# Narrow and wide matmuls of a seven-product up-projection, paired by channel tile

## The chip, the core and the metric

One core of a Trainium2 chip runs the whole block as one program. TensorE (PE in the profile) multiplies; its weight loads have a row of their own (PEld). VectorE (DVE), ScalarE (ACT) and GpSimd (POOL) work on the elements, SyncE (SP) issues most transfers. The metric is the device time of one execution in microseconds, as the median of three runs.

## The reference

A diffusion block on 512 latent tokens of width 2048: a mixer of two recurrent head groups, then a SwiGLU MLP with a 3x3 depthwise convolution on the gate branch, and a final norm. The change touches the MLP's up-projection only:

```python
def conv_ffn(h, rows, cols, w_up, conv_w, conv_b, w_down):
    b, t, _ = h.shape
    u = jnp.einsum('btd,df->btf', h, w_up)
    u_gate, u_val = jnp.split(u, 2, axis=-1)
    g = lax.conv_general_dilated(u_gate.reshape(b, rows, cols, D_FF), conv_w[:, :, None, :], ...)
    g = g.reshape(b, t, D_FF) + conv_b
    return jnp.einsum('btf,fd->btd', jax.nn.silu(g) * u_val, w_down)
```

Here t is 512, d is 2048 and f is 5504, which is 43 channel tiles of 128.

## The kernel before

**Two-part numbers.** To get float32 results from single-pass matmuls, each operand is split into a high part (a copy on ScalarE, line 90, that rounds) and a low part (the rest, a subtraction on VectorE, line 91). A product is then the sum of three: high x high, high x low and low x high.

**Seven products.** `up_seven(f)` makes the gate and the value of channel tile f, for f from 4 to 42. It halves the 16 tiles of 128 input channels (KH = 8 in a half), the 512 tokens (TH = 256 in a half) and the outputs (gate and value), and multiplies the resulting 2x2 blocks with seven products in place of eight, in Winograd's form: sums of token blocks are made once for the whole stage (`token_sums`), sums of weight blocks for every tile, by accumulating transfers and by two additions on VectorE. A product n takes a weight block of 8 pieces of 128x128, split into `wh` and `wl`, as the stationary operand, and as the moving one `operands[n](k)`, which holds the high part of 256 tokens in its first half and the low part in its second. So there are two kinds of matmul: a **narrow** one, `wl` against the high part (256 columns into the first half of the result), and a **wide** one, `wh` against both parts (512 columns into both halves). The halves are added later, with the combination of the products. In the profile the narrow ones read `lo_q` and the wide ones `hi_q`. The program issues all eight narrow ones, then all eight wide ones, into the same bank of PSUM (`x`, `w` or `v`).

**Order around it.** Tiles 4 to 38 and 40, 36 in all, also run a down block (`dn`, 48 matmuls of 512 columns) between their sixth and seventh product; 39, 41 and 42 don't. The product order is 0, 1, 3, 2, 5, 4, down block, 6 in the first kind and 0 to 6 in the second. Each engine takes its instructions in program order, which a scheduler sets from the program's text, its dependences and its priorities; splits and evacuations have high priority.

**Buffers.** The high parts rotate through three buffers in this stage (`hi_tile`), the low parts through two (`wlo`, tag `lo`), and the down block's weights use the same ones. A buffer is free when the last matmul that reads it is done.

The convolution (`conv`) is nine taps per tile, the first on ScalarE, eight on VectorE (line 1207). All matmuls of this stage show line 98, that of a helper.

Of the kernel before, what the change touches and what calls it, by code (L numbers as in the profile page):

```python
# [70 lines left out]
def block_kernel(ctx: ExitStack, tc: tile.TileContext, a: dict, out: bass.AP):  # L71
# [8 lines left out]
    def sub(o, x, y):  # L80
        V.tensor_tensor(out=o, in0=x, in1=y, op=ALU.subtract)
# [4 lines left out]
    def add(o, x, y):  # L86
        V.tensor_tensor(out=o, in0=x, in1=y, op=ALU.add)

    def split(hi, lo, x):
        split_ins[0] = S.copy(hi, x).ins  # L90
        return V.tensor_tensor(out=lo, in0=x, in1=hi.bitcast(F32), op=ALU.subtract).ins  # L91
# [5 lines left out]
    def mm(*args, **kw):  # L97
        ins = PE.matmul(*args, **kw)  # L98
        if pinned[0]:
            tc.keep_in_program_order(ins)  # L100
# [37 lines left out]
    def acc(name, shape=(P, T)):  # L138
        return psA.tile(list(shape), F32, name=name, tag="acc")

    def psb(name, shape=(P, T)):
        return psB.tile(list(shape), F32, name=name, tag="psb")
# [52 lines left out]
    def hi_tile(name, n):  # L195

        turn[0] += 1
        if third[0] and turn[0] % 3 == 0:
            return third[0].tile([P, 2 * T], F32R, name=name, tag="hi3")[:, 0:n]
        return whi.tile([P, n], F32R, name=name, tag="hi")  # L200
# [852 lines left out]
    for g in range(4):  # L1053
        if g:
            accs = unit(a["w_gates"][g], f"ga{g}", *hx)
        for i in range(4):
            k = 4 * g + i
# [53 lines left out]
    for n in range(4):  # L1111
        accs = unit(a["w_out"][n], f"wo{n}", yh, yl)
        with tc.high_priority():
            for i in range(4):
                k = 4 * n + i
# [12 lines left out]
    KH, TH = KT // 2, T // 2  # L1128
# [39 lines left out]
    def neg_add(o, x, y):  # L1168
        V.scalar_tensor_tensor(out=o, in0=x, scalar=-1.0, in1=y, op0=ALU.mult, op1=ALU.subtract)
# [27 lines left out]
    def conv(f, pad, val):  # L1197

        t = stage[1] if f < FIRST and f % 2 else tp.tile([P, T], F32, name=f"cv{f}", tag="cv")
        t3 = t.rearrange("p (r c) -> p r c", c=GW)  # L1200
        for tap in range(9):
            src = pad[:, tap // 3 : tap // 3 + ROWS, tap % 3 : tap % 3 + GW]
            w = cwt[:, f, tap : tap + 1]
            if tap == 0:
                S.activation(t3, src, AF.Identity, scale=w, bias=cbt[:, f : f + 1])  # L1205
            else:
                V.scalar_tensor_tensor(out=t3, in0=src, scalar=w, in1=t3, op0=ALU.mult, op1=ALU.add)  # L1207
        S.activation(t, t, AF.Silu)
        mul(t, t, val)
        gs[f] = [ytile(2 * (f % 8) + i, f"g{'hl'[i]}{f}", dtype=F32R) for i in range(2)]  # L1210
        split(*gs[f], t)

    def vtile(f):
        return stage[0] if f < FIRST and f % 2 else tp.tile([P, T], F32, name=f"val{f}", tag="val")
# [29 lines left out]
    def up_seven(f):  # L1244

        def load(q, i, j, **kw):
            eng = G if kw else nc.sync
            eng.dma_start(q, a["w_up"][f - FIRST, i, j].rearrange("p k c -> p (k c)"), **kw)  # L1248

        def block(n):  # L1250
            return wraw.tile([P, KH * P], F32, name=f"q{f}_{n}", tag="raw")

        s1, s3 = spare[0][:, f % 2, :], spare[1][:, 0, :]
        load(s1, 1, 0)
        a11 = block(0)
        load(a11, 0, 0)
        load(s1, 1, 1, accum_op=ALU.add)
        load(s3, 1, 0)
        a12 = block(1)
        load(a12, 0, 1)  # L1260
        load(s3, 0, 0, accum_op=ALU.add)

        def product(n, src, o, first):
            wh = hi_tile(f"hi_q{f}_{n}", KH * P)
            wl = wlo.tile([P, KH * P], F32R, name=f"lo_q{f}_{n}", tag="lo")
            with tc.high_priority():
                split(wh, wl, src)
            cs = [slice(P * k, P * k + P) for k in range(KH)]
            for k in range(KH):
                mm(o[:, 0, :], wl[:, cs[k]], operands[n](k)[:, 0], start=first and k == 0, stop=False,  # L1270
                   skip_group_check=True)
            for k in range(KH):
                mm(o, wh[:, cs[k]], operands[n](k), start=False, stop=k == KH - 1, skip_group_check=True)

        def rows(x):
            return x.rearrange("p (r c) -> p r c", c=GW)

        x = psb(f"x{f}", (P, 2, TH))
        w, v = (acc(f"{n}{f}", (P, 2, TH)) for n in "wv")
        pad, val = pads[f % 2], vtile(f)  # L1280

        def part(name, tag):
            return fp.tile([P, 2, TH], F32, name=f"{name}{f}", tag=tag)

        p1 = part("p1", "pa")

        def c11():
            add(p1, w, p1)
            add(pad[:, 1 : ROWS // 2 + 1, 1 : GW + 1], rows(p1[:, 0]), rows(p1[:, 1]))

        def c12():
            add(u2, v, u2)
            add(pad[:, ROWS // 2 + 1 : ROWS + 1, 1 : GW + 1], rows(u2[:, 0]), rows(u2[:, 1]))

        def c22():
            neg_add(p5, x, p5)
            add(val[:, hi], p5[:, 0], p5[:, 1])

        def c21():
            S.activation(val[:, lo], x[:, 0], AF.Copy, scale=-1.0)  # L1300
            sub(val[:, lo], val[:, lo], x[:, 1])

        def step(n, src, o, after):
            product(n, src, o, n in (0, 1, 3))
            with tc.high_priority():
                after()

        step(0, a11, x, lambda: S.copy(p1, x))
        step(1, a12, w, c11)
        with tc.high_priority():  # L1310
            add(a11, s1, a11)
            add(a12, a12, a11)
        p5, u2 = part("p5", "pa"), part("u2", "u2")
        steps = [(2, a11, x, lambda: S.copy(u2, x)), (3, s1, v, lambda: S.copy(p5, v)), (4, s3, x, c22), (5, a12, v, c12)]  # L1314
        for n in (1, 0, 3, 2) if f in DOWN else range(4):
            step(*steps[n])
        if f in DOWN:
            down_block(GROUPS[min(f // 4, 9) - 1], DOWN[f])
        a22 = block(2)
        load(a22, 1, 1)  # L1320
        step(6, a22, x, c21)
        conv(f, pad, val)
# [12 lines left out]
    def down_block(fs, blk):  # L1335
        accs = down_products(fs, blk)
        with tc.high_priority():
            for i in range(4):
                k = 4 * blk + i
                S.activation(stage[i], accs[i], AF.Copy, scale=modc[5][:, k : k + 1])  # L1340
                G.dma_start(x2d[k], stage[i], accum_op=ALU.add)
# [147 lines left out]
```

## Time and profile before

| what | us |
|---|---|
| median of 3 runs (lowest, highest) | 2479.32 (2476.03, 2481.27) |
| the profiled execution | 2478.88 |
| its span, first to last instruction | 2476.8 |
| VectorE's low splits of `q` buffers in the stage from 1240 to 2380, 191 of them | 230.6 busy |
| VectorE's eight taps of a tile in the same stretch, 306 of them | 229.2 busy |
| TensorE's idle time in the same stretch | 0.7 |

The stage with seven products a tile fills the stretch from about 1228 to 2380 us of the span. In the profile, a row of the time line gives the start, the time it lasts, the engine, the line, the operation and the tiles it writes and reads, and a count where equal rows are merged. A matmul's time there includes the fill and drain that the next one overlaps, so the distance of two starts, and not the duration, says what it costs.

### The profile page before, as it was taken

To read this page: it belongs to the slowest core of one execution; us is meant where nothing else is said; L and a number is where in the kernel's file an instruction comes from. 1 tells how busy PE (TensorE), PEld (TensorE's weight loads), DVE (VectorE), ACT (ScalarE), POOL (GpSimd) and SP (SyncE) were. 2 spreads that over 40 slices of the span, in tenths; PEclk is the share of its full clock that TensorE was granted. 3 is DMA by queue.
4 is the path that set the end of the run, shared out by engine and by line. 5 is a ranking of instruction groups with operands and counts; after the bars stand their busy time and mean duration, and the time that the engine had idled before them with its cause. 6 is when DMAs were issued, how large, how long until landed. Compare 5 with 4: busy or idle time off the path is not lost.

```text
span 2476.8 us, 35238 instructions
## 1 busy us (share of the span) xinstructions
PE 2439.1 (98%) x13610; PEld 2110.3 (85%) x13610; DVE 1752.0 (71%) x2472; ACT 1120.1 (45%) x1664; POOL 370.3 (15%) x362
## 2 busy tenths in 40 slices
PE   7999999999999999999999999999999999999998
PEld 4888899989998888888888888888888888888887
DVE  5566766555555688867887777777777777777884
ACT  4224544322323444435455555555555555555553
POOL 0000000000000344540011111111111111111101
PEclk9999999999999999999999999999999999999999
DMA  9751112124343878862588888888888888888762
GB/s 371 279 189 52 35 43 77 60 86 136 128 137 102 265 267 291 281 204 90 145 186 190 192 190 194 194 195 190 194 190 192 187 189 190 193 190 191 181 205 69
DMA packets 137913, 429.68 MB, mean 173 GB/s; under 512 B 15505, under 2 KB 19985, under 8 KB 137745
## 3 DMA queue, kind: packets, MB, share of 16 engines
q1 hardware_dynamic: 104688, 348.24, 42.8%
q0 software_dynamic: 31968, 78.66, 20.1%
q8 instruction: 107, 1.75, 0.3%
q10 hardware_dynamic: 1088, 0.52, 0.1%
q14 instruction: 62, 0.50, 0.1%
HBM read 381.22 MB, written 46.14 MB: 173 GB/s over the span
## 4 chain that ended last, share of the span: by engine, by line
PE 91%; issue 3%; DVE 3%; DMA 1%; ACT 0%; POOL 0%; SPq 0%; POOLq 0%; DVEq 0%; ACTq 0%
PE a L98 18%; PE x L98 17%; PE dn L98 16%; PE v L98 9%; PE wo L98 7%; PE ga L98 7%; PE w L98 4%; PE po L98 4%; PE u L98 4%; PE ps_m L98 1%; PE sl L98 1%; PE cst L98 1%; PE mc L325 1%; DMA xl<-in_xT 0%; PE s L98 0%
## 5 line engine op out<-in xcount | busy, mean ns | idle before, releaser
L91 DVE TENSOR_TENSOR lo_q<-q,hi_q 128x1024 fp32r<-128x1024 f32 x195 | 235.4, 1223 | 143.1 <-ACT spare L1340 117.6
L90 ACT CAST hi_q<-q 128x1024 fp32r<-128x1024 f32 x195 | 205.2, 1053 | 230.4 <-PE dn L98 162.0
L98 PE MATMUL dn<-gh,lo_d 128*128 128x512 f32 x660 | 257.6, 390 | 0.0
L98 PE MATMUL dn<-gl,hi_d 128*128 128x512 f32 x660 | 257.5, 390 | 0.0
L98 PE MATMUL dn<-gh,hi_d 128*128 128x512 f32 x660 | 257.5, 390 | 0.0
L1207 DVE SCALAR_TENSOR_TENSOR cv<-pad,cwt,cv 128x512 f32<-128x512 f32 x328 | 246.6, 752 | 6.3 <-ACT cv L1205 0.5
L98 PE MATMUL x<-bt,hi_q 128*128 128x512 f32 x936 | 235.4, 394 | 0.0
L98 PEld LDWEIGHTS x<-bt,hi_q 128*128 128x128 f32 x936 | 167.7, 188 | 30.7
L1248 POOL DMA_DIRECT2D spare<-in_w_up x78 | 68.7, 883 | 728.6 <-DMA spare<-in_w_up 647.4
L314 POOL TENSOR_TENSOR sumg_m<-sumg_m,raw_m 128x512 f32<-128x512 f32 x74 | 124.1, 1677 | 198.7 <-ACT raw_m L313 172.3
L98 PE MATMUL a<-hi_h,hTh 128*128 128x256 f32 x512 | 149.1, 291 | 0.0
L91 DVE TENSOR_TENSOR lo_d<-raw_d,hi_d 128x1024 fp32r<-128x1024 f32 x84 | 101.3, 1206 | 66.4 <-ACT hi_d L90 52.0
L306 DVE SCALAR_TENSOR_TENSOR sum_m<-raw_m,csil,sum_m 128x512 f32<-128x512 f32 x112 | 145.5, 1299 | 1.3
L98 PEld LDWEIGHTS dn<-gl,hi_d 128*128 128x128 f32 x660 | 124.0, 188 | 26.2 <-DVE gl L91 0.2
L98 PEld LDWEIGHTS dn<-gh,hi_d 128*128 128x128 f32 x660 | 123.9, 188 | 26.3 <-ACT gh L90 0.4
L98 PEld LDWEIGHTS dn<-gh,lo_d 128*128 128x128 f32 x660 | 124.0, 188 | 26.1
L98 PE MATMUL a<-lo_h,hTh 128*128 128x256 f32 x512 | 145.0, 283 | 0.0
L98 PE MATMUL a<-hi_h,hTl 128*128 128x256 f32 x512 | 145.0, 283 | 0.0
L91 DVE TENSOR_TENSOR lo_q<-spare,hi_q 128x1024 fp32r<-128x1024 f32 x78 | 95.3, 1222 | 56.3 <-ACT hi_q L90 56.3
L98 PEld LDWEIGHTS x<-bt,lo_q 128*128 128x128 f32 x936 | 125.7, 188 | 10.3 <-ACT u L1314 1.1
L90 ACT CAST hi_h<-raw_h 128x1024 fp32r<-128x1024 f32 x64 | 67.0, 1047 | 137.9 <-PE a L98 129.7
L98 PE MATMUL x<-bt,lo_q 128*128 128x256 f32 x936 | 128.2, 279 | 0.7 <-ACT u L1314 0.7
(371 smaller groups left out, 5872.3 us busy)
## 6 DMA issues: line engine op xcount, KB each, us to landing
raw_m<-in_w_mod SPq DMA_DIRECT2D x192, 512.0 KB, 4.9
q<-in_w_up SPq DMA_DIRECT2D x117, 512.0 KB, 4.7
raw_d<-in_w_down SPq DMA_DIRECT2D x81, 512.0 KB, 4.1
spare<-in_w_up SPq DMA_DIRECT2D x78, 512.0 KB, 4.5
spare<-in_w_up POOLq DMA_DIRECT2D x78, 512.0 KB, 7.3
raw_h<-in_w_heads SPq DMA_DIRECT2D x64, 512.0 KB, 3.5
x2d<-stage POOLq DMA_DIRECT2D x72, 256.0 KB, 5.1
x2d<-spare POOLq DMA_DIRECT2D x72, 256.0 KB, 5.1
```

The costliest lines, as they stand in the source:

```text
L90: split_ins[0] = S.copy(hi, x).ins
L91: return V.tensor_tensor(out=lo, in0=x, in1=hi.bitcast(F32), op=ALU.subtract).ins
L98: ins = PE.matmul(*args, **kw)
L306: V.scalar_tensor_tensor(out=parts["v"], in0=raw[:, 0, :], scalar=ce, in1=parts["v"], op0=ALU.mult, op1=ALU.add)
L314: G.tensor_tensor(out=parts["g"], in0=parts["g"], in1=raw[:, 1, :], op=ALU.add)
L325: tc.keep_in_program_order(PE.matmul(ps[:, i : i + 1], po[:, P * i : P * i + P], cst[:, C_ONE : C_ONE + 1], start=True, stop=True))
L1207: V.scalar_tensor_tensor(out=t3, in0=src, scalar=w, in1=t3, op0=ALU.mult, op1=ALU.add)
L1248: eng.dma_start(q, a["w_up"][f - FIRST, i, j].rearrange("p k c -> p (k c)"), **kw)
```

## The change

The second `for k` line goes away, so that the loop body issues the narrow matmul of piece k and then the wide one of the same piece:

```diff
             for k in range(KH):
                 mm(o[:, 0, :], wl[:, cs[k]], operands[n](k)[:, 0], start=first and k == 0, stop=False,
                    skip_group_check=True)
-            for k in range(KH):
                 mm(o, wh[:, cs[k]], operands[n](k), start=False, stop=k == KH - 1, skip_group_check=True)
```

The number of instructions of each kind is the same. What moves is their order. On TensorE, at the start of tile 13 (the stage's tenth), there stands before, with `b00` and `b1` as token operands and the number behind `q` as the tile and the product:

```order
L98 MATMUL x13_12847<-b00_9578,lo_q13_0_12853 128x256 x8
L98 MATMUL x13_12847<-b00_9578,hi_q13_0_12852 128x512 x8
L98 MATMUL w13_12848<-b1_9580,lo_q13_1_12874 128x256 x8
L98 MATMUL w13_12848<-b1_9580,hi_q13_1_12873 128x512 x8
L98 MATMUL v13_12849<-bt0_9581,lo_q13_3_12900 128x256 x8
```

On TensorE at the same place there now stands, for the first half of product 0:

```order
L98 MATMUL x13_12847<-b00_9578,lo_q13_0_12853 128x256
L98 MATMUL x13_12847<-b00_9578,hi_q13_0_12852 128x512
L98 MATMUL x13_12847<-b00_9578,lo_q13_0_12853 128x256
L98 MATMUL x13_12847<-b00_9578,hi_q13_0_12852 128x512
L98 MATMUL x13_12847<-b00_9578,lo_q13_0_12853 128x256
L98 MATMUL x13_12847<-b00_9578,hi_q13_0_12852 128x512
```

The runs of eight have become single rows that alternate; the order of the products is the same as before in every tile but tile 4, where product 5 now stands ahead of product 4's last pair.

VectorE's order moves too, since the scheduler sees the low buffer in use for longer. From the start of tile 13, before (`q13_0` and `q13_1` are the raw weight blocks, `spare` a sum of two, `val12` and `cv12` the value and the convolution of the tile ahead):

```order
L91 TENSOR_TENSOR lo_q13_0_12853<-q13_0_12840,hi_q13_0_12852 128x1024
L91 TENSOR_TENSOR lo_q13_1_12874<-q13_1_12844,hi_q13_1_12873 128x1024
L87 TENSOR_TENSOR q13_0_12840<-spare_10516,q13_0_12840 128x1024
L81 TENSOR_TENSOR val12_12592<-val12_12592,x12_12589 128x256
L87 TENSOR_TENSOR q13_1_12844<-q13_1_12844,q13_0_12840 128x1024
L91 TENSOR_TENSOR lo_q13_3_12900<-spare_10516,hi_q13_3_12899 128x1024
L84 TENSOR_TENSOR cv12_12823<-cv12_12823,val12_12592 128x512
L91 TENSOR_TENSOR lo_q13_2_12921<-q13_0_12840,hi_q13_2_12920 128x1024
```

And VectorE's rows at the same place now:

```order
L91 TENSOR_TENSOR lo_q13_0_12853<-q13_0_12840,hi_q13_0_12852 128x1024
L87 TENSOR_TENSOR q13_0_12840<-spare_10516,q13_0_12840 128x1024
L91 TENSOR_TENSOR lo_q13_1_12874<-q13_1_12844,hi_q13_1_12873 128x1024
L81 TENSOR_TENSOR val12_12592<-val12_12592,x12_12589 128x256
L87 TENSOR_TENSOR q13_1_12844<-q13_1_12844,q13_0_12840 128x1024
L84 TENSOR_TENSOR cv12_12823<-cv12_12823,val12_12592 128x512
L91 TENSOR_TENSOR lo_q13_3_12900<-spare_10516,hi_q13_3_12899 128x1024
L91 TENSOR_TENSOR gl12_12836<-cv12_12823,gh12_12835 128x512
L91 TENSOR_TENSOR lo_q13_2_12921<-q13_0_12840,hi_q13_2_12920 128x1024
```

The splits of products 1, 3 and 2 have each gone down behind one more row of other work, and of the convolution's taps two more stand ahead of product 0's split.

Late in the stage, VectorE's rows in tile 40, from the split for product 4 to the first one for the down block, before (`cv39` is the convolution of tile 39, whose own loop had no down block):

```order
L91 TENSOR_TENSOR lo_q40_4_19858<-spare_10516,hi_q40_4_19857 128x1024
L1207 SCALAR_TENSOR_TENSOR cv39_19717<-pad1_9572,cwt_9567,cv39_19717 128x512 x2
L91 TENSOR_TENSOR lo_d32_3_19885<-raw_d32_3_19883,hi_d32_3_19884 128x1024
L87 TENSOR_TENSOR u240_19792<-v40_19743,u240_19792 128x512
L84 TENSOR_TENSOR cv39_19717<-cv39_19717,val39_19558 128x512
```

And VectorE's rows there now:

```order
L91 TENSOR_TENSOR lo_q40_4_19858<-spare_10516,hi_q40_4_19857 128x1024
L1207 SCALAR_TENSOR_TENSOR cv39_19717<-pad1_9572,cwt_9567,cv39_19717 128x512 x3
L87 TENSOR_TENSOR u240_19792<-v40_19743,u240_19792 128x512
L91 TENSOR_TENSOR lo_d32_3_19885<-raw_d32_3_19883,hi_d32_3_19884 128x1024
L87 TENSOR_TENSOR pad0_9571<-u240_19792 128x4x64
```

One tap and one addition more stand ahead of the down block's split. The order of transfers on SP and POOL is the same as before; ScalarE's is but for a few swaps of neighbours.

## The prediction

> **What bounds the kernel now.** I read three views in this order: the page (busy shares, the chain that ended last), the busy time by stretches over the stage that the change touches, and the time line of TensorE (PE) over one channel tile there.
>
> ```profile
> PE 2439.1 (98%) x13610; PEld 2110.3 (85%) x13610; DVE 1752.0 (71%) x2472; ACT 1120.1 (45%) x1664; POOL 370.3 (15%) x362
> PE 91%; issue 3%; DVE 3%; DMA 1%; ACT 0%; POOL 0%; SPq 0%; POOLq 0%; DVEq 0%; ACTq 0%
> core 0: us, PE busy (x) PEld busy (x) DVE busy (x) ACT busy (x) POOL busy (x), PEclk, DMA share, GB/s
> 1600.00:2000.00 400.00, 400.00 (x2114) 344.26 (x2113) 304.31 (x370) 208.03 (x263) 69.25 (x79) 1.00 0.83 191
> ```
>
> The chain is TensorE for 91%, and the stretch shows why: in 400 us of the up-projection's seven-product stage TensorE is busy for all 400.00 at a granted clock of 1.00, while VectorE (DVE) has a quarter of its time free. Whatever leaves the spacing of TensorE's instructions alone and lets nobody come late leaves the time alone. So the question is the spacing, and one tile shows it:
>
> ```profile
> 1499.78 0.39 PE L98 MATMUL dn<-gh,hi_d 128*128 128x512 f32 x1
> ...
> 1500.23 0.39 PE L98 MATMUL dn<-gh,lo_d 128*128 128x512 f32 x1
> 1500.46 1.11 PE L98 MATMUL x<-bt,lo_q 128*128 128x256 f32 x8
> 1501.41 2.04 PE L98 MATMUL x<-bt,hi_q 128*128 128x512 f32 x8
> 1503.28 1.10 PE L98 MATMUL x<-b,lo_q 128*128 128x256 f32 x8
> 1504.22 2.00 PE L98 MATMUL x<-b,hi_q 128*128 128x512 f32 x8
> 1506.06 1.10 PE L98 MATMUL w<-b,lo_q 128*128 128x256 f32 x8
> 1507.01 2.00 PE L98 MATMUL w<-b,hi_q 128*128 128x512 f32 x8
> 1508.85 1.10 PE L98 MATMUL v<-bt,lo_q 128*128 128x256 f32 x8
> 1509.79 1.99 PE L98 MATMUL v<-bt,hi_q 128*128 128x512 f32 x8
> 1511.61 1.10 PE L98 MATMUL x<-bt,lo_q 128*128 128x256 f32 x8
> 1512.55 2.00 PE L98 MATMUL x<-bt,hi_q 128*128 128x512 f32 x8
> 1514.39 1.11 PE L98 MATMUL v<-b,lo_q 128*128 128x256 f32 x8
> 1515.34 2.00 PE L98 MATMUL v<-b,hi_q 128*128 128x512 f32 x8
> 1517.17 1.07 PE L98 MATMUL x<-bt,lo_q 128*128 128x256 f32 x8
> 1518.08 2.00 PE L98 MATMUL x<-bt,hi_q 128*128 128x512 f32 x8
> 1519.91 0.39 PE L98 MATMUL dn<-gh,hi_d 128*128 128x512 f32 x1
> ```
>
> The first column is the start, and matmuls overlap, so I take starts from starts. The seven products (6 of the tile before, then 0, 1, 3, 2, 5, 4) go from 1500.46 to 1519.91: 19.45 us for 7 x 8 pairs of a narrow (256 columns) and a wide (512) matmul, **347.3 ns a pair**. The eight narrow ones of a product take 0.95, 0.94, 0.95, 0.94, 0.94, 0.95 and 0.91 us: 6.58 in all, 117.5 ns each. The wide take 12.87, or 229.8 each. No product starts late.
>
> **The change part by part.** No instruction is added or removed; the eight narrow matmuls of a product are put between its eight wide ones, 39 tiles x 7 products x 8 = 2184 pairs. Two things follow: TensorE alternates, and the low weight buffer is held longer.
>
> *Spacing.* First, what a crossing from narrow to wide costs today. One matmul's own time is the middle of three figures here (shortest, median, longest):
>
> ```profile
> L98 PE MATMUL x<-b,lo_q x312: 275/280/283, 1228.5 to 2362.3; 128*128 128x256 f32 x156
> L98 PE MATMUL x<-b,hi_q x312: 387/393/398, 1229.4 to 2364.1; 128*128 128x512 f32 x156
> ```
>
> A row's length less one matmul's own (0.28 narrow, 0.393 wide) is the seven steps inside a run; the rest up to the next row is the crossing. Over the seven products: narrow 7.69 - 1.96 = 5.73 us for 49 inner steps, 117 ns, and 6.58 - 5.73 = 0.85 for seven crossings, 121. Wide: 14.03 - 2.75 = 11.28 for 49, 230, and 12.87 - 11.28 = 1.59 for seven, 227. A crossing pair is 348, an inner pair 347, with some 3 ns of rounding. So the crossing itself is free, and after the change all steps but a product's last are crossings.
>
> Second, what each width takes when it is left alone for long:
>
> ```profile
> 142.82 0.28 PE L98 MATMUL a<-hi_h,hTh 128*128 128x256 f32 x1
> 145.69 0.34 PE L98 MATMUL a<-hi_h,hch 128*128 128x384 f32 x1
> ```
>
> Between these two stand 24 narrow matmuls of the head projection, the first included: 2.87 us, 119.6 ns each. Three wide ones of the down projection ahead of the tile above take 1500.46 - 1499.78 = 0.68, 227 ns each. Their sum is 346.6, against 347.3 in the products: there the narrow runs are 2.1 ns a matmul faster than that and the wide runs 2.8 slower, so what one run gains the next gives back. I read that as an array that takes the columns at a fixed rate plus a fixed charge, in whatever order. New spacing: 119.6 + 227 = 346.6, **2184 x -0.7 ns = -1.5 us**.
>
> *The weight loads.* A hope could be that a wide matmul covers the loads of two.
>
> ```profile
> 1500.24 1.12 PEld L98 LDWEIGHTS x<-bt,lo_q 128*128 128x128 f32 x8
> 1501.29 1.71 PEld L98 LDWEIGHTS x<-bt,hi_q 128*128 128x128 f32 x8
> ```
>
> The first low load starts at 1500.24, when the matmul ahead of its own started (1500.23); the first high one at 1501.29, when the last narrow matmul did (1501.41 less one step). Each load is exactly one matmul ahead. With that depth a narrow matmul still has one load beside it, a wide one too, in either order: nothing gained. The Trainium skill ("TensorE: Matmul & The Clock Gate", Step-by-step: what each phase is for) says that the queue pulls weight loads ahead of matmuls in flight, through a background buffer; its section Back-to-back issue gap gives N/2.4 + 2.5 ns for a lone matmul, by which a pair would be an estimated 325 ns and the change worth -49 us. The rows here show one load ahead and no narrow step under 113 ns, so the sum does not go by it.
>
> *The low buffer.* There are two, and the split that fills one is VectorE's. Until now product n frees its buffer after its eighth narrow matmul, from now on one wide matmul before its end, 1.6 us later (seven wide steps). Behind a split that waits, all of VectorE's queue waits. I walk the tile above in the new order of VectorE's rows, with the steps of these:
>
> ```profile
> 1500.72 2.36 DVE L91 TENSOR_TENSOR lo_q<-q,hi_q 128x1024 fp32r<-128x1024 f32 x2 [3.46 <-ACT spare L1340]
> 1503.00 1.22 DVE L87 TENSOR_TENSOR q<-spare,q 128x1024 f32<-128x1024 f32 x1
> 1504.13 0.42 DVE L81 TENSOR_TENSOR val<-val,x 128x256 f32<-128x256 f32 x1
> 1504.46 1.22 DVE L87 TENSOR_TENSOR q<-q,q 128x1024 f32<-128x1024 f32 x1
> 1505.60 1.22 DVE L91 TENSOR_TENSOR lo_q<-spare,hi_q 128x1024 fp32r<-128x1024 f32 x1
> ```
>
> A step of 1024 columns is 1.14, of 256 is 0.33, of 512 about 0.6. Product 0's split starts at 1500.72 as before, since it waits for the last down matmul (1500.23 + 0.39). The sum of weights follows, to 1503.0. Product 1's split now waits for product 6's last narrow matmul: 1503.28 - 0.23 - 0.12 + 0.28 = 1503.2, so it ends at 1504.4; TensorE wants it at 1506.06. Then val (1504.7), the second sum (1505.8), a multiply (1506.45), and product 3's split, whose buffer is free at 1506.06 - 0.35 + 0.28 = 1506.0: it ends at 1507.7 and is wanted at 1508.85. That is the least cover of the tile, **1.1 us**, where it was 2.0; the later products have 1.3 to 1.6. Cost: nothing. Its other side: each 0.1 us beyond the cover would cost 39 x 0.1 = 4 us. The tiles without a down block (39, 41, 42) are tighter for VectorE:
>
> ```profile
> 2320.04 2.32 DVE L1207 SCALAR_TENSOR_TENSOR cv<-pad,cwt,cv 128x512 f32<-128x512 f32 x3
> 2322.80 1.07 PE L98 MATMUL v<-b,lo_q 128*128 128x256 f32 x8
> 2328.32 0.40 PE L98 MATMUL dn<-gh,hi_d 128*128 128x512 f32 x1
> ```
>
> In tile 40 product 4's split can start when product 2 ends, 2322.8; with its 1.14, three taps (2.23), an add (0.6) and its own 1.22, the down block's first split then ends at 2328.0, for 2328.32. Cover 0.3 us at one place; a miss is some tenths once, so nothing again. Transfers keep their order, ScalarE's rows too but for swaps of neighbours, and the raw buffers are let go up to 1 us later, less than what a split waits ahead of TensorE.
>
> *Sum.* The profiled execution took 2478.88 us (span 2476.8 and 2.1 around it); less 1.5 is 2477.4. The median of the runs shown is 2479.32, 0.4 above it: **2477.8**.
>
> **The rivals.**
>
> *A. Every narrow matmul is cheap behind a wide one.* Product 4's narrow run took 0.91 us, 113.75 each (1517.17 to 1518.08), and it came behind a wide run like all others, so the 117.5 elsewhere isn't a floor. If each narrow step goes to 113.75 and each wide one to the 227 of the down block, a pair is 340.75: 2184 x -6.6 = -14.3 us, **2465**. For it: the wide steps of all seven runs are above 227 (1.82 us for eight at the least). Against: in the long narrow run of the heads the steps rise to 119.6. A narrow step without any charge, 227 - 119.6 = 107, would be -29 us and is the bound below.
>
> *B. Every wide matmul is dear behind a narrow one.* The first wide ones of a run start late:
>
> ```profile
> 1501.65 0.40 PE L98 MATMUL x<-bt,hi_q 128*128 128x512 f32 x1
> 1501.88 0.40 PE L98 MATMUL x<-bt,hi_q 128*128 128x512 f32 x1
> 1502.12 0.40 PE L98 MATMUL x<-bt,hi_q 128*128 128x512 f32 x1
> ```
>
> Product 6's first three steps are (1502.12 - 1501.41)/3 = 237 ns, 10 above the down block. If alternation makes each wide step such a first one, at 237 and 230 (the inner mean) say 234, a pair is 118 + 234 = 352: 2184 x 4.7 = +10 us, **2490**. Against it: the first wide steps cost more only where the narrow ones cost less, and the tile's total fits the free-standing widths.
>
> *C. The low buffer turns into a wait (slower).* Place: product 3's split in each of 36 tiles with a down block. It decides once VectorE gets there over 1.1 us later than in my walk, for example if the multiply ahead of it waits for ScalarE's activation. At 0.3 us beyond, 39 x 0.3 = +12 us, **2491**. Against it: between product 1's split and this one nothing waits in my walk, and 0.5 us of the cover would survive even if VectorE did a whole 512-column row more.
>
> **How the numbers follow.** A measurement of this kernel tells about 0.2%, 5 us, from no change. My forecast (2474.3 to 2484.3, spacing kept within 2.3 ns a pair) gets 0.48, A 0.30, B 0.16, C 0.06. So faster 0.30, same 0.48, slower 0.22; the time is that of the first. The range reaches to A's 2465 less 3 and to C's 2491 plus 1; what lies beyond (A's bound of 107 ns, B at 237 throughout) is less than 2 in 10. The forecast's own range is those 5 us on each side.
>
> **What would show it.** In the profile after: a tile's seven products still 19.4 us from the first start to the down block's first (A: 19.1, B: 19.7); TensorE busy 400.00 of 400; low splits that start right after the product two ahead of theirs ends, with more of VectorE's waiting put down to PE; no gap ahead of `v<-bt`, the fourth product of the row above. I am wrong if narrow and wide steps, one beside the other, do not add up to what they add up to apart, or if a split comes after its product is due.

## The result, and the profile after

The median went from 2478.88 us (five runs, 2476.03 to 2481.27) to **2488.07 us** (five runs, 2485.99 to 2489.11): a ratio of 1.0035 (95% interval 1.0024 to 1.0046), 9.2 us slower. That lies inside the outer range of the prediction (2462 to 2492), above the forecast's own 2474.3 to 2484.3, and on the other side: 1.5 us less was forecast.

The page of the changed kernel, its busy times and its chain:

```profile
PE 2445.0 (98%) x13610; PEld 2111.0 (85%) x13610; DVE 1765.0 (71%) x2472; ACT 1112.4 (45%) x1664; POOL 370.6 (15%) x362
PE 95%; DVE 3%; DMA 1%; issue 1%; ACT 0%; SPq 0%; DVEq 0%; ACTq 0%
```

The busy time of the same stretch of the stage:

```profile
core 0: us, PE busy (x) PEld busy (x) DVE busy (x) ACT busy (x) POOL busy (x), PEclk, DMA share, GB/s
1600.00:2000.00 400.00, 400.00 (x2099) 342.74 (x2098) 307.62 (x368) 204.54 (x263) 68.42 (x78) 1.00 0.82 189
```

TensorE is still busy for all 400.00 us at a clock of 1.00, and got through 2099 matmuls of the records where it had 2114. Nobody makes it wait; the same matmuls stand further apart. TensorE's time line over the tile of the prediction shows it (the first four matmuls, then the first of each later product and of the down block; the first column is the start):

```profile
1501.44 0.28 PE L98 MATMUL x<-bt,lo_q 128*128 128x256 f32 x1
1501.56 0.39 PE L98 MATMUL x<-bt,hi_q 128*128 128x512 f32 x1
1501.79 0.28 PE L98 MATMUL x<-bt,lo_q 128*128 128x256 f32 x1
1501.90 0.40 PE L98 MATMUL x<-bt,hi_q 128*128 128x512 f32 x1
...
1504.25 0.28 PE L98 MATMUL x<-b,lo_q 128*128 128x256 f32 x1
...
1507.07 0.28 PE L98 MATMUL w<-b,lo_q 128*128 128x256 f32 x1
...
1509.90 0.28 PE L98 MATMUL v<-bt,lo_q 128*128 128x256 f32 x1
...
1512.71 0.28 PE L98 MATMUL x<-bt,lo_q 128*128 128x256 f32 x1
...
1515.50 0.28 PE L98 MATMUL v<-b,lo_q 128*128 128x256 f32 x1
...
1518.29 0.28 PE L98 MATMUL x<-bt,lo_q 128*128 128x256 f32 x1
...
1521.09 0.39 PE L98 MATMUL dn<-gh,hi_d 128*128 128x512 f32 x1
```

The seven products take 1521.09 - 1501.44 = 19.65 us, where they took 19.45. From the unrounded starts, averaged over tiles 10 to 38, which repeat to 1 ns, it is 19.645 against 19.454: 0.191 x 39 = 7.4 us. The products are not alike: the second and third (0 and 1) take 2.82 and 2.83, the fifth and sixth (2 and 5) 2.79.

One us more is at the stage's first tile, which the prediction did not walk. TensorE's rows there that wait, after, and then before (the brackets give the idle time before the row and what ended it):

```profile
1239.80 0.35 PE L98 MATMUL x<-bt,lo_q 128*128 128x256 f32 x1 [1.23 <-DVE lo_q L91]
...
1247.92 0.50 PE L98 MATMUL dn<-gh,lo_d 128*128 128x512 f32 x1 [0.42 <-DVE lo_d L91]
```

```profile
1240.69 0.51 PE L98 MATMUL x<-bt,lo_q 128*128 128x256 f32 x2 [0.67 <-ACT u L1314]
```

1.23 + 0.42 - 0.67 = 1.0 us, once, and these are all the waits that TensorE has in the stage. The row at 1239.80 is product 4's first. Its split begins 11.4 us after the stage's first matmul where it began 9.9 us after it: VectorE works there without a gap of 0.1 us in either run, and now has two more taps (0.66 us each) ahead of this split. The wait belongs to the change: the runs below with the same pairs and the same weights (`second_half`, `shift4`, `kick`) show the same 1.2 and 0.4 us.

Together 8.4 us; the stage from its first to its last product grew by 8.7 (1152.2 to 1160.8). The rest lies mostly in the last four tiles, whose products took 0.23 to 0.35 us longer. The two spans differ by only 7.2 (2484.0 and 2476.8); what lies outside the stage was 1.5 shorter in this execution, less than the spread of the runs.

The other signs came as forecast. The weight loads (PEld) are one matmul ahead still:

```profile
1501.45 0.19 PEld L98 LDWEIGHTS x<-bt,hi_q 128*128 128x128 f32 x1
1501.56 0.19 PEld L98 LDWEIGHTS x<-bt,lo_q 128*128 128x128 f32 x1
```

The load for the wide matmul of 1501.56 starts when the narrow one of 1501.44 does. VectorE's waits in the stage (us in all, times, longest), after, and then the two largest of the low splits before:

```profile
DVE lo_q L91 <- PE dn L98: 64.6, 34, 1.9
DVE lo_q L91 <- PE x L98: 57.1, 38, 1.9
```

```profile
DVE lo_q L91 <- ACT spare L1340: 117.6, 34, 3.5
DVE lo_q L91 <- ACT hi_q L90: 76.2, 73, 1.7
```

The splits used to wait for ScalarE and now wait for TensorE to release the buffer. They still come in time; VectorE's time line has the splits of products 0, 1 and 3:

```profile
1501.70 1.22 DVE L91 TENSOR_TENSOR lo_q<-q,hi_q 128x1024 fp32r<-128x1024 f32 x1 [1.91 <-PE dn L98]
...
1504.27 1.23 DVE L91 TENSOR_TENSOR lo_q<-q,hi_q 128x1024 fp32r<-128x1024 f32 x1
...
1507.48 1.22 DVE L91 TENSOR_TENSOR lo_q<-spare,hi_q 128x1024 fp32r<-128x1024 f32 x1
```

Product 1's split ends at 1505.50 for 1507.07, a cover of 1.6 us as in the prediction's walk; product 3's ends at 1508.70 for 1509.90, 1.2 where the walk had 1.1.

### The profile page after: what moved, and what is told of

Its sections match the earlier page's. It is cut to its first block, busy times and chain, and to the rows that moved or that the text cites. A ratio compares the mean times of both kernels' runs of the same rounds, so it can differ in the third digit from the quotient of the medians.

```text
span 2484.0 us, 35236 instructions
## 1 busy us (share of the span) xinstructions
PE 2445.0 (98%) x13610; PEld 2111.0 (85%) x13610; DVE 1765.0 (71%) x2472; ACT 1112.4 (45%) x1664; POOL 370.6 (15%) x362
## 4 chain that ended last, share of the span: by engine, by line
PE 95%; DVE 3%; DMA 1%; issue 1%; ACT 0%; SPq 0%; DVEq 0%; ACTq 0%
PE a L98 18%; PE dn L98 18%; PE x L98 17%; PE v L98 9%; PE wo L98 7%; PE ga L98 7%; PE w L98 4%; PE po L98 4%; PE u L98 4%; PE ps_m L98 1%; PE sl L98 1%; PE dl L98 1%; PE cst L98 1%; PE mc L325 1%; PE s L98 0%
## 5 line engine op out<-in xcount | busy, mean ns | idle before, releaser
L98 PE MATMUL x<-bt,hi_q 128*128 128x512 f32 x936 | 332.9, 395 | 0.0
L98 PE MATMUL x<-bt,lo_q 128*128 128x256 f32 x936 | 262.2, 280 | 1.2 <-DVE lo_q L91 1.2
L98 PEld LDWEIGHTS x<-bt,hi_q 128*128 128x128 f32 x936 | 176.0, 188 | 40.8
L98 PEld LDWEIGHTS x<-bt,lo_q 128*128 128x128 f32 x936 | 175.9, 188 | 2.9 <-ACT u L1313 1.5
```

## The experiments

All measure one thing: the seven products of a tile, from the first start to the down block's (mean over tiles 10 to 38, from the records). "Step" is from one matmul's start to the next one's. The kernel before has 19.454 us, the change 19.645; each 0.1 us is 3.9 us of the kernel.

The theories as they came up: **S**, each change between narrow and wide has a fixed price; **R**, short runs are dear, only longer ones get cheap; **H**, the price is for adding to the PSUM half that the matmul ahead has just added to; **O**, it is for reading the same operand columns twice running; **W**, it is for taking weights from two buffers in turn; **P**, no order has a price of its own: a step depends on where on a fine time grid the matmul starts, and that is handed on from matmul to matmul.

### How long the runs are

```diff
-            for k in range(KH):
-                mm(o[:, 0, :], wl[:, cs[k]], ...)
-                mm(o, wh[:, cs[k]], ...)
+            for b in range(0, KH, 4):
+                for k in range(b, b + 4):
+                    mm(o[:, 0, :], wl[:, cs[k]], ...)
+                for k in range(b, b + 4):
+                    mm(o, wh[:, cs[k]], ...)
```

Four narrow, four wide, twice:

> Four narrow matmuls, then four wide ones, twice a product. A tile's seven products took 19.45 us with runs of eight and 19.65 with pairs (first start to the down block's first start). Theory S (each change of width costs the same, 14 more of them a product made +27 ns): 2 more a product, 19.48 us a tile, time +1 us over before. Theory R (a wide run is dear for its first two or three matmuls and cheap after, whatever the narrow ones do): 19.55 or more, +4 us. Theory H (narrow and wide meet in the same half of the PSUM bank): goes with the number of meetings, as S.

Measured: 19.541 us; 2482.1 against 2478.98, ratio 1.0013 (1.0003 to 1.0022). Between the two numbers, nearer to R.

The same with 2 in place of 4, so two narrow and two wide, four times:

> Two narrow, two wide, four times a product. Theory S: 6 more changes of width a product than runs of eight, 19.53 us a tile, +3 us over before. Theory R: as dear as pairs or dearer, 19.65, +8 us. Theory H: as S.

Measured: 19.365 us; 2477.17, ratio 0.9993 (0.9984 to 1.0001). Four changes from narrow to wide a product where before the change there was one, and *less* time for the tile (the kernel's own time does not tell it from the one before): S and R both fall. TensorE's time line has a hint in it (the start of the tile, the first part of product 1, and the tile's end):

```profile
1502.08 0.40 PE L98 MATMUL x<-bt,lo_q 128*128 128x256 f32 x2
...
1507.61 0.40 PE L98 MATMUL w<-b,lo_q 128*128 128x256 f32 x2
1507.85 0.62 PE L98 MATMUL w<-b,hi_q 128*128 128x512 f32 x2
1508.31 0.39 PE L98 MATMUL w<-b,lo_q 128*128 128x256 f32 x2
1508.54 0.62 PE L98 MATMUL w<-b,hi_q 128*128 128x512 f32 x2
1508.99 0.28 PE L98 MATMUL w<-b,lo_q 128*128 128x256 f32 x1
...
1521.44 0.39 PE L98 MATMUL dn<-gh,hi_d 128*128 128x512 f32 x1
```

The first two narrow ones take 0.24 us and the next two 0.23, the wide ones behind them 0.46 and 0.45: the same four matmuls, twice, at different prices. In mean steps it is 120 118 229 231, then 114 113 226 229 ns, and again.

### Wide ahead of narrow

```diff
-                mm(o[:, 0, :], wl[:, cs[k]], ...)
-                mm(o, wh[:, cs[k]], ...)
+                mm(o, wh[:, cs[k]], ...)
+                mm(o[:, 0, :], wl[:, cs[k]], ...)
```

> Pairs with the wide matmul ahead of its narrow one. Theory S: the same number of changes, 19.65 us a tile, time as with pairs (+9 us over before). A theory in which the moving operand's repetition matters (the wide one reads again what the narrow one has just read): still repeated, 19.65 too. A theory in which the low part's lateness matters: below 19.65, since the first matmul of a product then needs the high part alone.

Measured: 19.717 us; 2490.61, ratio 1.0049 (1.0036 to 1.0061), slower yet, though the two orders differ only at the ends of a product.

### Which half of PSUM, which operands

```diff
-                mm(o[:, 0, :], wl[:, cs[k]], ...)
+                mm(o[:, 1, :], wl[:, cs[k]], ...)
```

> Pairs as in the change, but the narrow matmul adds to the second half of the PSUM bank's result, not the first (the halves are summed later, so the sum is the same). Theory H (a narrow matmul and the start of the wide one behind it add to the same columns one after the other): back to 19.45 us a tile, time as before. Theories S, R and those of weights and operands: 19.65, +9 us.

Measured: 19.645 us and the same steps as the change; 2488.06, ratio 1.0035 (1.0023 to 1.0048). H falls.

```diff
+                j = (k + 4) % KH
                 mm(o[:, 0, :], wl[:, cs[k]], operands[n](k)[:, 0], ...)
-                mm(o, wh[:, cs[k]], operands[n](k), ...)
+                mm(o, wh[:, cs[j]], operands[n](j), ...)
```

> Pairs as in the change, but the narrow matmul of piece k stands beside the wide one of piece k+4 (modulo 8): the same order of kinds, other operands side by side. Theory P (the step of a matmul is set by its kind, its neighbours' kinds and the place of its start on a grid of 6.67 ns, so the order of kinds alone fixes the path): 19.645 us a tile again, step for step. Theory O (the wide matmul suffers from reading the operand that the narrow one has just read): towards 19.45.

```profile
1503.16 0.28 PE L98 MATMUL x<-bt,lo_q 128*128 128x256 f32 x1
...
1522.81 0.39 PE L98 MATMUL dn<-gh,hi_d 128*128 128x512 f32 x1
```

Measured: 2487.81 in a single run beside 2478.5, and on TensorE's time line 1522.81 - 1503.16 = 19.65 us. O falls as well.

### Which weight buffer

The narrow matmul takes its weights from the high buffer, so this kernel leaves the low weights out of the products:

```diff
-                mm(o[:, 0, :], wl[:, cs[k]], ...)
+                mm(o[:, 0, :], wh[:, cs[k]], ...)
```

> Pairs, but the narrow matmul takes its weights from the high buffer too, the same piece as the wide one (the low weights are left out of the products). Theory W (taking weights from two buffers in turn is what costs): back to 19.45 us a tile or under. Theory P: the widths alternate as before, so some repeating cycle of pairs remains, 349 to 353 ns a pair, 19.55 to 19.75 us a tile.

Measured: 2485.89 in a single run; 19.633 us, almost the change's time. But two products of its time line differ (the first row is product 1, from 1506.32 to 1509.15; the second product 3, to 1511.92):

```profile
1506.32 2.99 PE L98 MATMUL w<-b,hi_q 128*128 128x256 f32 x16
1509.15 0.63 PE L98 MATMUL v<-bt,hi_q 128*128 128x256 f32 x3
...
1511.92 0.86 PE L98 MATMUL x<-bt,hi_q 128*128 128x256 f32 x4
```

2.83 us against 2.77. Products 6, 3 and 4, every third one, whose high weights lie in the last of the three high buffers (`hi_tile` takes them in turn, nine a tile), settle at steps of 117 and 230 ns; the others go on with 118 231, 118 233, 123 237. So two buffers in turn are not what costs the change its time, but which buffer it is goes with the steps. At the first tile VectorE's rows stand as before the change here, and so does TensorE's wait (0.7 us for ScalarE's `u`): the 1.0 us more goes with the use of the low buffer and the row order that follows from it, not with the pairs.

Both matmuls wide, so that only the alternation of weights is left (the low weights then also multiply the low operands, 56 x 256 columns more a tile), first in runs of eight and then in pairs:

```diff
-                mm(o[:, 0, :], wl[:, cs[k]], operands[n](k)[:, 0], ...)
+                mm(o, wl[:, cs[k]], operands[n](k), ...)
```

> Every narrow matmul is made wide (it then adds low weights times low operand too), in runs of eight. All theories: wide steps of 227 to 231 ns, 25.4 to 25.9 us for a tile's seven products; the reference for the run with pairs.

> Every narrow matmul is made wide, and low and high weights alternate. Theory W: dearer than the same in runs by the change's 27 ns a product, 0.19 us a tile. Theories S and P: width does not alternate, so it takes what the runs of eight take, within 0.05 us a tile.

Measured: 25.634 us in runs and 25.722 in pairs (2717.66 and 2721.69, one run each), +0.088. Less than half of W's 0.19, and a little more than the 0.05 of S and P. It comes from products 6, 3 and 4 (3698, 3680, 3680 ns against 3661, 3659, 3659) and the one behind 6 (3677 against 3663); product 1 takes 6 ns less, and products 2 and 5 are the same to the nanosecond. With the run before, W falls as the cause of the 0.19.

### The same order, entered differently

The steps of each place in a tile, as means in ns, N narrow and W wide, and their sum (from the records of these kernels; from tile 10 to tile 38 no place's step moves by more than 3 ns):

```
before, product 4   N 114 113 113 113 113 113 113 113  W 233 236 228 233 231 227 227 226   2746
before, product 5   N 120 117 118 118 117 117 118 117  W 229 232 226 229 232 226 229 232   2778
change, product 1   118 233 123 237 118 231 118 233 123 237 118 231 118 233 123 237        2831
change, product 3   118 232 119 229 118 238 118 232 119 229 117 238 117 232 119 229        2805
change, product 5   119 229 120 229 118 232 119 229 120 229 117 232 119 229 120 229        2791
change, product 4   118 231 117 233 121 233 112 233 121 233 112 233 121 233 112 233        2799
```

The change's own products already show four cycles for one order of matmuls: two among those with the third high buffer (3 and 4), two among the others (1 and 5). And the length of every cycle that repeats is a whole number of one small time:

```
cycle                                    sum, ns   / 6.667
wide run     226 229 232                   686.7    103.0
narrow run   113 113 113 113               453.1     68.0
pairs        123 237 118 231 118 233      1060.0    159.0
pairs        119 229 118 238 118 232      1053.3    158.0
pairs        120 229 118 232 119 229      1046.7    157.0
pairs        121 233 112 233               700.0    105.0
pairs, one weight buffer  117 230 117 230  693.3    104.0
two and two  120 117 229 232 113 114 226 229  1380.0  207.0
```

The tiles agree: in every one of these kernels the time from one tile's first start to the next tile's (tiles 10 to 38, one tile of `kick` left out) is a whole number of 6.667 ns, to 0.1 ns; 30346.64 ns is 4552.0 of them before, 30539.93 is 4581.0 after.

P reads this so: the same three pairs cost 1046.7 or 1060.0 ns, and which of them a product gets is settled by where on a grid of 6.67 ns it starts. If so, a change in one product must alter the time of *other* products that nobody touched. Only product 6, the first of a tile, gets another order for its last six matmuls (`NWNWNWNWNWWNNWWN`); all others remain pairs:

```diff
-            for k in range(KH):
-                mm(o[:, 0, :], wl[:, cs[k]], ...)
-                mm(o, wh[:, cs[k]], ...)
+            for i, kind in enumerate(ORDER[n]):
+                k = done[kind]
...
+                if kind == "N":
+                    mm(o[:, 0, :], wl[:, cs[k]], ...)
+                else:
+                    mm(o, wh[:, cs[k]], ...)
```

> All products in pairs as in the change, but in product 6, the first of a tile's seven, the last six matmuls stand wide, wide, narrow, narrow, wide, wide, narrow in place of alternating (narrow, wide five times, then these with one more narrow between). Products 0 and 1 keep their order of pairs; with the change they take 2.82 and 2.83 us, while products 2 and 5, in the same order, take 2.79. Theory P (the step depends on where in a grid of 6.67 ns a matmul starts, so one product hands its phase to the next): products 0 and 1 together fall from 5.65 to 5.58 us though nothing in them is changed. Theories that charge a crossing, a buffer or an operand a fixed price: 5.65 again, only product 6 differs.

TensorE's time line (the starts of products 6, 0, 1 and 3):

```profile
1503.58 0.28 PE L99 MATMUL x<-bt,lo_q 128*128 128x256 f32 x1
...
1506.37 0.28 PE L99 MATMUL x<-b,lo_q 128*128 128x256 f32 x1
...
1509.15 0.28 PE L99 MATMUL w<-b,lo_q 128*128 128x256 f32 x1
...
1511.95 0.28 PE L99 MATMUL v<-bt,lo_q 128*128 128x256 f32 x1
```

Products 0 and 1, from 1506.37 to 1511.95, take 5.58 us; in the change they took 1509.90 - 1504.25 = 5.65. Not one of their instructions, buffers or operands is different. In means 2789 and 2791 ns against 2822 and 2831, on the cycle of 1046.7 and no longer that of 1060.0, in each of tiles 10 to 38. Products 3 and 4, equally untouched, went the other way, from 2805 to 2812 and from 2799 to 2811. A fixed price for anything *in* the pairs gives 5.65; P had said 5.58. What this shows is that a product's time depends on what the product ahead hands on; that it is a place on a time grid is inferred from the cycles' lengths. The tile falls to 19.577 us, and a single run gave 2486.58 beside a median of 2478.84.

### Orders picked by their steps

With the steps seen so far as a table (next step by kind, neighbours and the place on the grid), orders can be picked for a low sum. Each product its own order, by the same loop:

```
ORDER (0 to 6) = WNNNNNNNNWWWWWWW WWNNNNNNNNWWWWWW NNNWWNNNNNWWWWWW NNNNNNNNWWWWWWWW
                 WNNNNNNNNWWWWWWW NNNWWWWWWNNNNNWW NWNWWWWWNNNNNWNW
```

> Each of the seven products gets an order of its own, chosen from a table of steps by phase that was gathered from the traces so far, so that narrow matmuls fall on the phase where they take 113 ns and wide runs on 226, 229, 232. Theory P: 19.23 us for a tile's seven products, against 19.45 in runs of eight and 19.65 in pairs: 39 x -0.22 = -8.7 us, 2470. If the table does not carry over to orders that it has not seen: between 19.3 and 19.6, 2473 to 2485. Theory S: about 5 changes of width a product, 19.5 us, 2481.

Measured: 19.337 us; 2476.24, ratio 0.9987 (0.9978 to 0.9996). Products 1, 2, 3 and 5 went to 2741, 2754, 2746 and 2742 ns, but 0 and 4, both with a wide one ahead of eight narrow, to 2779 and 2807: the table had no such entry at that phase and forecast the tile 0.1 us too low. The -8.7 us did not come; 2.6 did, inside what was expected if the table does not carry over.

A second choice:

```
ORDER (0 to 6) = NNWWWWWWNNNNWWNN WWNNNNNNNNWWWWWW WWWNNNNNNWWWWWNN NNNNNNNNWWWWWWWW
                 NNNNNNNNWWWWWWWW WWNNNNNNNNWWWWWW NNNWWWWWWWNNWNNN
```

> Another choice from the same table. Theory P: 19.22 us a tile, -9 us, 2470. If the table does not carry over: 19.3 to 19.6, 2473 to 2485. Theory S: as phase_a, 2481.

Measured: 19.414 us; 2477.48, ratio 0.9993 (0.9985 to 1.0002). The table missed by 0.19 here, and again the -9 us did not come. Product 1 has the same order in both kernels, `WWNNNNNNNNWWWWWW`, and took 2741 ns in the first and 2784 in this one; in this one product 5 has it too and took 2741.

One order for all seven, `NNNWWNNNNNWWWWWW` (three narrow, two wide, five narrow, six wide):

> One order for all products: three narrow, two wide, five narrow, six wide. Theory P by the same table: 19.33 us a tile, -5 us, 2474. Theory S: 4 changes of width a product, 19.48, 2480.

```profile
1500.30 0.52 PE L99 MATMUL x<-bt,lo_q 128*128 128x256 f32 x3
...
1503.08 0.52 PE L99 MATMUL x<-b,lo_q 128*128 128x256 f32 x3
1503.43 0.62 PE L99 MATMUL x<-b,hi_q 128*128 128x512 f32 x2
1503.89 0.73 PE L99 MATMUL x<-b,lo_q 128*128 128x256 f32 x5
1504.46 1.54 PE L99 MATMUL x<-b,hi_q 128*128 128x512 f32 x6
1505.83 0.50 PE L99 MATMUL w<-b,lo_q 128*128 128x256 f32 x3
...
1519.63 0.39 PE L99 MATMUL dn<-gh,hi_d 128*128 128x512 f32 x1
```

Measured: 19.334 us (1519.63 - 1500.30 = 19.33), as P's table had it; **2473.66, ratio 0.9978** (0.9969 to 0.9987). The five narrow matmuls in the middle of product 0 take 1504.46 - 1503.89 = 0.57 us, 113 ns each; those of products 2, 3 and 4 do too, those of 6, 1 and 5 take 115 to 120. That beats both kernels, by 5.2 us the one before and by 14.4 the change, with the same instructions.

## Why the prediction went wrong, point by point

- **The bound: right.** TensorE runs back to back at a granted clock of 1.00, before and after; of the 8.4 us found, all but 1.0 are in its spacing.
- **The weight loads: right.** One ahead, in either order, and no pair under 340 ns.
- **The low buffer: right in the steady tiles** (covers of 1.6 and 1.2 us for 1.6 and 1.1), and rival C did not come. Its walk began at tile 13; in the first tile of the stage 1.0 us more was lost to VectorE's splits, which came two taps later. Tile 40, where it left 0.3 us, cost no wait.
- **The spacing: wrong, and this is the step that failed:** "I read that as an array that takes the columns at a fixed rate plus a fixed charge, in whatever order". It gave -0.7 ns a pair, -1.5 us. Measured: 350.8 ns a pair (19.645 us / 56) where the mean tile had 347.4 (19.454 / 56), so +3.4 ns (a narrow step went from 117.2 to 118.6 in the mean, a wide one from 230.1 to 232.2) and +7.4 us. The steps do depend on the order, and not by a price for crossings. The crossing pair of 348 ns ahead of it came from rows rounded to 10 ns; by the records the last narrow step of a run takes 116.8 and the last wide one 228.5, a pair of 345.3, and these stand at the end of runs, not in alternation. The down block's 227 and the heads' 119.6 were values of long runs too. The numbers were in the trace of before: product 4's narrow run at 113.75 beside 117.5 elsewhere, which the prediction used for rival A, already said that equal work had two prices.
- **Rival B had the size (352 ns, +10 us) and not the mechanism.** Not every wide matmul behind a narrow one is dear: in the change's product 5 they take 229, 229 and 232 in turn, in its product 1 233, 237 and 231, and the two and two order takes 229 and 226 at the first wide one. That the size came near is luck. The first steps of 237 in product 6 of before were that product's alone; product 5's were 229, 232 and 226.
- **Rival A** took the narrow price of 113.75 as open to every order. It can be had, and in the run of five of the last experiment four of seven products had it; in the change's pairs it came only as 121 and 112 in turn.

Open is what in the chip makes the grid, why the third high buffer leads to other cycles, and the full table of steps: the one drawn up from the runs missed two of seven products, and more in the second choice. P as stated is not the whole: in the last kernel products 0 and 3 have one order and come to their last run behind five narrow steps of 113.3 ns, at the same place on the grid (1.67 and 1.64 ns past a multiple of 6.667 ns, counted from the tile's first start), and the first wide step then takes 225.8 ns in product 0 and 232.5 in product 3, whose high weights lie in the third buffer.

## What to carry to other kernels

Where matmuls with fresh weights run back to back, don't take their spacing for a sum of widths: the same sixteen took 2.74 to 2.83 us here by their order, by what ran ahead of them and by the buffer of their weights. So look at the step of every place in a period, not at means over runs; where one order shows two prices, take a reordering as worth some tenths of a per cent with either sign (the orders here gave -0.2 to +0.5), and run a few. An edit that is no loss where it is made can show up in a product that wasn't touched.

## What the chip showed that was not expected

- A repeating cycle of matmul steps takes a whole number of 6.67 ns, to within 0.3 ns, in all eight cycles shown, while most single steps do not: 512 columns took 224 to 241 ns and 256 columns 112 to 123, all with new weights.
- One order of pairs ran at 346.7, 348.9, 350, 351.1 and 353.3 ns a pair, by phase and by weight buffer.
- A change in one product moved two others by 73 ns of 5653, tile after tile.
- With one order and one place on the grid, a wide step took 225.8 ns with one weight buffer and 232.5 with another.
